# A planner's table of durations in a two-layer trunk (windowed attention, gated DeltaNet): measured times on all engines, a shared port, one load queue

## The chip, the core and the metric

The kernel runs on one core of one Trainium2 chip. A core has five engines that run their own instruction streams side by side: TensorE (PE in the profile; matmuls, with its weight loads shown as PEld), VectorE (DVE), ScalarE (ACT), GpSimd (POOL) and SyncE (SP), which issues the DMA transfers here. They meet only through semaphores. The metric is the device time of one execution in microseconds (us), given as the median of several runs; one further execution is recorded by the profiler.

## The reference

Two decoder layers over a prompt of 1024 tokens and a sample group of 8 sequences of 4 tokens, with 1024 features, all in float32. Each layer computes

```python
x = x + gate(c) * Branch(rms_norm(x) * (1 + scale(c)) + shift(c))
```

with shift, scale and gate from `silu(c) @ w_mod + b_mod`. Every branch has one input projection, which also yields a gate path z, and one output projection of `branch_output * silu(z)`.

Layer 0's branch is attention with 16 query and 4 key heads of 64: each query sees itself and the 128 positions before it (a learned sink per head joins the softmax); the sample group's queries see a cache of 128 positions. Layer 1's branch is gated DeltaNet: q, k and v pass a causal convolution over 4 tokens and SiLU, q and k are normalised, and each of 16 value heads (two to a q/k head) carries a 128 x 128 state S:

```python
S_t = exp(g_t) * S_{t-1} + k_t u_t^T
u_t = beta_t * (v_t - (exp(g_t) * S_{t-1})^T k_t)
o_t = S_t^T q_t / sqrt(128)
```

It is done by chunks: inside a chunk a unit lower triangular system is solved, and a scan over the chunks carries S. After the layers a last norm follows. Outputs are the tokens of both groups, the new key and value caches, the new convolution tails and the new states.

## The kernel before, in words

**Tiling.** Tokens lie on the free axis during projections: 1056 tokens (1024 + 32) in groups of 384, 384 and 288. A float32 product of full precision is made of three matmuls on operands split in a high and a low part: `wh x hhi`, `wh x hlo`, `wl x hhi` (rows `ps_pj<-h2hi,wh` and so on in the profile). Weights come in by DMA (`wr`), ScalarE rounds them to `wh` and GpSimd subtracts to get `wl`.

**Layer 1.** The 16 value heads are 8 pairs, `hq` 0 to 7. For each pair there are: `solve` (L1834), which builds the triangular blocks of eight chunks of 128 tokens in tiles UZ; `invert` (L1884), which inverts all 32 x 32 diagonal blocks of a pair at once on VectorE, in a tile X, in 31 steps of two instructions (`tmp<-X`, a product, and `X<-X,tmp`, a subtraction; the 31 pairs are the 62 instructions of which the prediction speaks); `diagonal` and `blocks` (L1938), which put these inverses back (`Xd`, VectorE's STREAM_TRANSPOSE into UZ) and build the off-diagonal blocks by small matmuls (`ps_lg<-UZ,M`) that VectorE copies into UZ; `decayed`, `chain` (L1986), the scan over the eight chunks, in each of which a matmul with UZ gives u, VectorE scales it to `us`, TensorE multiplies it with k (`ps_mi<-us,ktok`), and VectorE updates S; `output` and `gating` (`vo`, `mo`, `zl`). Before the last stage (the output projection, `out_y_p<-xt`) come the sample group's states, `S<-in_state_gdn_s`, which are loaded once for products with q and k (KQT, cK, cQ) and once more for their update.

**What sets the order of the work.** The program is written by Python generators, here called jobs. `weave(gen, name, hq)` (L487) puts a job in a list sorted by a rank out of the tables `K` and `KR` (L241). After each projection matmul `stages()` (L498) resumes every job whose condition is true; `until(cond)` (L509) stops the projections until a condition holds, and resumes only jobs. Conditions are of two kinds: counts (`finished[0] >= r - 1`, L2173: the chain of pair r - 1 is done before the k projection of pair r + 1 goes on), and times of a planner. The planner is the class `Core`: each instruction issued through it passes a helper (L89, the line that nearly all rows of the profile bear), and `Core.issued` (L111) adds its estimated duration to a clock `free[engine]` and notes when each tile was `written` and last `used`. `ready(tile)` holds when the tile's planned time is not after TensorE's clock, `soon(tile)` allows 0.4 us and `idle(engine, tile)` 0.8 us beyond. In the order in which they are issued the instructions are then bound, engine by engine, by dependencies with the reason "program order". So the planner's durations don't alter any instruction; they decide where each one stands in its engine's stream. The inversion's steps, for example, each wait on `yield idle("vector")`.

The durations before, in short: a fixed part and a rate for each engine (VectorE 0.08 us and 960 elements per us and partition, GpSimd 0.02 or 0.14 us and 420, a DMA 2.4 us whatever its size), with 0.1 us from an instruction to the next that needs it on the same engine and 0.2 us to another engine.

`cached` (L1036) is the job that opens the sample group's attention against the cache (loads `kc`, `vc`) once the prompt's attention is done.

## Time and profile before

| | |
|---|---|
| runs: median (lowest to highest) | 1736.98 us (1735.34 to 1741.25), 3 runs |
| the profiled execution | 1732.34 us |
| its span on the core | 1730.6 us |
| TensorE busy | 1621.2 us (94%), 10666 instructions |
| VectorE, ScalarE, GpSimd busy | 1174.6, 862.6 and 675.5 us |
| mean granted TensorE clock | 0.982 |
| moved by DMA | 191.82 MB |

Rows of the profile read: start, duration, engine, line, operation, `out<-in`, partitions x elements, count; a bracket at the end gives the time that the engine had stood idle before, and what released it. In rows of a wait the three numbers are total time, times and longest. Rows by stretch of time give, for each engine, the busy time and the count of instructions in it. TensorE's matmuls are pipelined, so that a duration can be longer than the distance to the next start.

### The profile page before, as it was taken

What the parts mean: (1) busy time and instruction counts of PE and PEld (TensorE: products, weight loads), DVE (VectorE), ACT (ScalarE), POOL (GpSimd) and SP (SyncE); (2) the same over time, 40 slices, a digit from 0 to 9 for tenths busy, and PEclk for the clock granted to TensorE, in tenths of its full rate; (3) what the DMA queues carried; (4) which work ended last, traced back from release to release, by engine and by line L of the source; (5) the groups of instructions that cost most, each with busy time, mean ns of one, the idle gap of its engine ahead of it and who ended that gap; (6) DMA issues with size and microseconds to landing.
All of it is one profiled execution on the core that took longest, in us unless ns stands there. A gap on an engine that the chain in (4) does not pass through costs nothing. (4 is left out here: it accounts for less than half of the span.)

```text
span 1730.6 us, 32224 instructions
## 1 busy us (share of the span) xinstructions
PE 1621.2 (94%) x10666; PEld 1429.5 (83%) x10666; DVE 1174.6 (68%) x3538; ACT 862.6 (50%) x2514; POOL 675.5 (39%) x1576
## 2 busy tenths in 40 slices
PE   6999999999999999589999999999999998989897
PEld 5987888977788889469989999899999996657675
DVE  4426675555565787757878778778697776357676
ACT  5625555453335664166554655554655655332332
POOL 2601121122213356235544654546356565323332
PEclk9999999999999999799999999999999999999998
DMA  9542122234233323122412324224132237764885
GB/s 330 153 133 73 51 58 55 51 103 114 92 122 97 105 55 85 29 68 69 127 42 73 102 58 114 65 69 117 46 104 70 56 93 227 218 190 138 244 268 171
DMA packets 281577, 191.82 MB, mean 111 GB/s; under 512 B 98361, under 2 KB 253881, under 8 KB 281378
## 3 DMA queue, kind: packets, MB, share of 16 engines
q1 hardware_dynamic: 281410, 189.75, 38.2%
q8 instruction: 85, 1.39, 0.3%
q14 instruction: 82, 0.67, 0.1%
HBM read 144.68 MB, written 47.04 MB: 111 GB/s over the span
## 5 line engine op out<-in xcount | busy, mean ns | idle before, releaser
L89 POOL TENSOR_TENSOR wl<-wr,wh 128x128 fp32r<-128x128 f32 x488 | 236.7, 515 | 485.5 <-ACT wh L89 449.4
L89 PE MATMUL ps_pj<-h2hi,wh 128*128 128x384 f32 (+1 forms) x1128 | 379.9, 337 | 0.0
L89 PE MATMUL ps_pj<-h2lo,wh 128*128 128x384 f32 (+1 forms) x1128 | 378.1, 335 | 0.0
L89 PE MATMUL ps_pj<-h2hi,wl 128*128 128x384 f32 (+1 forms) x1128 | 376.8, 334 | 0.0
L89 PEld LDWEIGHTS ps_pj<-h2hi,wh 128*128 128x128 f32 x1128 | 213.2, 189 | 3.1 <-ACT wh L89 0.2
L89 PEld LDWEIGHTS ps_pj<-h2hi,wl 128*128 128x128 f32 x1128 | 213.2, 189 | 2.7 <-POOL wl L89 0.2
L89 PEld LDWEIGHTS ps_pj<-h2lo,wh 128*128 128x128 f32 x1128 | 213.0, 189 | 2.2
L89 POOL TENSOR_TENSOR xt<-xt,y 128x512 f32<-128x512 f32 (+1 forms) x48 | 63.6, 1328 | 194.3 <-DVE y L89 170.4
L89 PE MATMUL ps_pj<-hlo,wh 128*128 128x384 f32 (+1 forms) x360 | 119.1, 331 | 0.0
L89 PE MATMUL ps_pj<-hhi,wh 128*128 128x384 f32 (+1 forms) x360 | 118.4, 329 | 0.0
L89 PE MATMUL ps_pj<-hhi,wl 128*128 128x384 f32 (+1 forms) x360 | 118.1, 328 | 0.0
L89 DVE SCALAR_TENSOR_TENSOR vT<-XR,cT,vT 128x384 f32<-128x384 f32 (+1 forms) x144 | 83.9, 591 | 47.4 <-ACT vT L89 45.3
L89 DVE TENSOR_TENSOR tmp<-X 64x31 f32<-64x31 f32 (+15 forms) x248 | 89.0, 359 | 16.9 <-POOL X L89 13.4
L89 DVE TENSOR_TENSOR X<-X,tmp 64x31 f32<-64x31 f32 (+15 forms) x248 | 90.7, 366 | 8.5
L89 ACT CAST wh<-wr 128x512 fp32r<-128x512 f32 x122 | 75.1, 617 | 16.4 <-PE ps_pj L89 11.3
L89 POOL TENSOR_TENSOR Xd<-Xc,cst 32x128 f32<-32x128 f32 x128 | 62.7, 490 | 40.5 <-DVE UZ L89 24.4
L89 PEld LDWEIGHTS ps_pj<-hlo,wh 128*128 128x128 f32 x360 | 67.7, 188 | 10.5 <-issue 10.5
L89 ACT COPY XR<-ps_pj 128x384 f32<-128x384 f32 (+1 forms) x96 | 43.0, 448 | 59.5 <-PE ps_pj L89 59.4
L89 PEld LDWEIGHTS ps_pj<-hhi,wh 128*128 128x128 f32 x360 | 67.7, 188 | 4.0 <-issue 3.1
L89 ACT ACTIVATE prob<-prob,nm 128x256 f32<-128x256 f32 (+1 forms) x128 | 62.2, 489 | 15.5 <-DVE nm L89 15.3
L89 PEld LDWEIGHTS ps_pj<-hhi,wl 128*128 128x128 f32 x360 | 67.7, 188 | 2.2 <-issue 2.1
L89 ACT ACTIVATE qe<-ps_mi,Eg 128x128 f32<-128x128 f32 x112 | 34.9, 363 | 60.4 <-PE ps_mi L89 60.3
(574 smaller groups left out, 4203.9 us busy)
## 6 DMA issues: line engine op xcount, KB each, us to landing
wr<-in_gdn_w_in SPq DMA_DIRECT2D x96, 256.0 KB
S<-in_state_gdn_s SPq DMA_DIRECT2D x40, 256.0 KB
xt<-in_x_prompt SPq DMA_DIRECT2D x16, 512.0 KB
wm<-in_w_mod SPq DMA_DIRECT2D x16, 512.0 KB
wr<-in_swa_w_in SPq DMA_DIRECT2D x64, 128.0 KB
wmod<-in_w_mod SPq DMA_DIRECT2D x32, 256.0 KB
wm<-in_w_mod SPq DMA_DIRECT2D x32, 256.0 KB
DP<-gcr SPq DMA_DIRECT2D x64, 128.0 KB
```

Of the source, the lines that this page charges most:

```text
L89: inst = fn(*args, **kwargs)
```

## The change

`Core` prices instructions in a new way; nothing else but one condition is touched.

- `issued` calls a function for each engine. `on_tensor`: 0.174 us for 384 columns in the fast format (0.164 before), 0.14 us more where tiled and untiled matmuls change over, double durations for the first 4 us after TensorE has been idle for over 2.2 us, and 0.165 us until the result is there. `on_scalar`: smaller fixed parts, 0.09 us for a scale or bias per partition, 0.093 for an accumulated sum, 1.29 us to change the function table, 0.1 us until the result. `on_vector`: other fixed parts, the double rate for all `tensor_scalar` forms from SBUF, 0.08 us until the result, and an instruction with two operands from SBUF (or at the double rate) starts only after a GpSimd instruction that is planned to run at that time. `on_gpsimd`: memsets have a price, and an instruction starts only after such a VectorE instruction.
- Loads and stores share one queue in the planner: each takes a time by its size and its longest run of adjacent bytes, and lands no sooner than 2.0 us after it starts.
- The step from one instruction to the next that needs it is `GO`, 0.035 us (0.05 from a DMA, none from TensorE to TensorE), in place of 0.1 and 0.2.
- `cached` also waits until the job `modulate` is over.

```diff
--- before.py
+++ after.py
@@ -76,6 +76,9 @@
 CONST, COFF = constants()
 
 
+GO = 0.035
+
+
 class Engine:
 
 
@@ -100,7 +103,8 @@
         self.tc, self.nc = tc, tc.nc
         self.free, self.last = {}, {}
         self.written, self.used, self.slots, self.parts, self.wide = {}, {}, {}, set(), {}
-        self.group = 0
+        self.group, self.full, self.slow, self.table, self.queue = 0, True, 0.0, 0, 0.0
+        self.pool, self.port = [], []
         for e in ("tensor", "scalar", "vector", "gpsimd", "sync"):
             self.free[e] = 0.0
             setattr(self, e, Engine(self, e))
@@ -115,42 +119,106 @@
         n = 1
         for d in outs[0].shape[1:]:
             n *= d
-        start = self.free[eng]
+        start = base = self.free[eng]
         for a in srcs:
             start = max(start, self.after(self.written, a, eng))
             if a.space == PSUM:
                 start = max(start, self.after(self.used, a, eng))
         for a in outs:
-            if self.used.get(self.key(a), (0.0, ""))[1] != "sync" or eng != "sync":
-                start = max(start, self.after(self.used, a, eng))
+            t, e = self.used.get(self.key(a), (0.0, eng))
+            if e != eng or eng not in ("tensor", "sync"):
+                start = max(start, t + GO)
         if "dma" in op:
+
             self.free[eng] = start + 0.45
-            end = start + 2.4
+            size = outs[0].shape[0] * n if outs[0].space != DRAM else int(np.prod(outs[0].shape))
+            part = min(4 * self.run(outs[0]), 4 * self.run(srcs[0]), 4096)
+            self.queue = max(self.queue, start + 0.9) + size * 4 / part * (8.5 + part * 0.0375) * 7e-5
+            end = done = max(start + 2.0, self.queue + 1.0)
         else:
-            rate, fixed = {"tensor": (2400 if op == "matmul" and srcs[0].dtype == F32R
-                                      else 1200 if op == "transpose" else 600, 0.004),
-                           "scalar": (1200, 0.06 if op == "copy" and srcs[0].space == PSUM else 0.14
-                                      if srcs and srcs[0].space == PSUM else 0.18),
-                           "vector": (960, 0.13 if op == "scalar_tensor_tensor" else 0.08),
-                           "gpsimd": (420, 0.02 if n >= 256 else 0.14)}[eng]
-            if op == "matmul" and outs[0].shape[0] <= 64 and srcs[0].dtype == F32:
-                rate = 2400 if n <= 64 and outs[0].shape[0] <= 32 else 600 * P / outs[0].shape[0] if self.group != outs[0].offset // outs[0].ap[0][0] else rate
-            if eng == "tensor":
-                self.group = outs[0].offset // outs[0].ap[0][0]
-            if op == "tensor_scalar_mul" and srcs and srcs[0].space != PSUM and eng == "vector":
-                rate = 1920
-            if op == "memset":
-                rate = 1e9
-            end = self.free[eng] = start + fixed + n / rate
+            start, dur, late = getattr(self, "on_" + eng)(op, start, base, n, outs, srcs, args, kwargs)
+            self.free[eng], end, done = start + dur, start + dur + late, start + dur + 0.02
             if eng in self.last:
                 self.tc.add_manual_dep(ins, self.last[eng],
                                        mybir.DependencyInfo(mybir.DependencyClass.NoSync, mybir.DependencyReason.DATA),
                                        reason="program order")
             self.last[eng] = ins.name
         for a in srcs:
-            self.used[self.key(a)] = max(self.used.get(self.key(a), (0.0, "")), (end, eng))
+            self.used[self.key(a)] = max(self.used.get(self.key(a), (0.0, "")), (done, eng))
         for a in outs:
             self.written[self.key(a)] = self.used[self.key(a)] = (end, eng)
+
+    @staticmethod
+    def run(a):
+
+        r = 1
+        for step, count in reversed(list(a.ap) if a.space == DRAM else list(a.ap)[1:]):
+            if count == 1:
+                continue
+            if step != r:
+                break
+            r *= count
+        return r
+
+    def on_tensor(self, op, start, base, n, outs, srcs, args, kwargs):
+        if start - base > 2.2:
+            self.slow = 4.0
+        rows = outs[0].shape[0]
+        tiled = rows <= 64 and srcs[0].dtype == F32 and op == "matmul"
+        group = outs[0].offset // outs[0].ap[0][0]
+        if tiled:
+            dur = 2 * (n / 1200 + 0.004)
+            if group != self.group:
+                dur = max(0.014, dur * rows / P)
+        elif srcs[0].dtype == F32R:
+            dur = max(0.108, n / 2400 + 0.014)
+        else:
+            dur = (1 if op == "transpose" else 2) * max(0.108, n / 1200 + 0.003)
+        if tiled == self.full:
+            dur += 0.14
+        self.group, self.full = group, not tiled
+        half = min(dur, self.slow)
+        self.slow -= half
+        return start, dur + half, 0.165
+
+    def on_scalar(self, op, start, base, n, outs, srcs, args, kwargs):
+        fixed = 0.05 if srcs and srcs[0].space == PSUM else 0.095
+        if op == "activation":
+            func = args[2] if len(args) > 2 else kwargs.get("func")
+            table = 1 if func in (AF.Exp, AF.Tanh) else 2 if func == AF.Silu else 0
+            if table and table != self.table:
+                start += 1.29 if self.table else 0.0
+                self.table = table
+        if hasattr(kwargs.get("scale"), "tensor") or hasattr(kwargs.get("bias"), "tensor"):
+            fixed += 0.09
+        if kwargs.get("accum_out") is not None:
+            fixed += 0.093
+        return start, fixed + n / 1200, 0.1
+
+    def on_vector(self, op, start, base, n, outs, srcs, args, kwargs):
+        scaled = op.startswith("tensor_scalar")
+        rate = 1920 if scaled and (not srcs or srcs[0].space != PSUM) else 960
+        fixed = 0.13 if op == "scalar_tensor_tensor" or scaled and len(srcs) > 1 else 0.1 if op == "transpose" else 0.075
+        dur = 0.0 if op == "memset" else fixed + n / rate
+
+        ins = [a for a in args[1:] if hasattr(a, "tensor")] + [a for k, a in kwargs.items() if hasattr(a, "tensor") and k not in ("out", "accum_out")]
+        big = sum(a.space != PSUM and np.prod(a.shape[1:]) >= max(2, n // 2) for a in ins)
+        if big > 1 or big and rate == 1920:
+            for x, y in reversed(self.pool[-12:]):
+                if x <= start < y:
+                    start = y
+            self.port.append((start, start + dur))
+        return start, dur, 0.08
+
+    def on_gpsimd(self, op, start, base, n, outs, srcs, args, kwargs):
+        dur = 0.03 + n / 1150 if op == "memset" else 0.14 + n / 470 if n < 256 else 0.03 + n / 420
+        if op != "memset" and n < 256 and outs[0].shape[-1] == P and outs[0].dtype == F32R:
+            dur = 0.41
+        for x, y in self.port[-12:]:
+            if x <= start < y:
+                start = y
+        self.pool.append((start, start + dur))
+        return start, dur, 0.045
 
     def key(self, a):
 
@@ -160,7 +228,7 @@
 
     def after(self, table, a, eng):
         t, e = table.get(self.key(a), (0.0, eng))
-        return t + (0.0 if e == eng == "tensor" else 0.1 if e == eng else 0.2)
+        return 0.0 if e == eng == "tensor" else t + (0.05 if e == "sync" else GO)
 
     def slot(self, key, bufs, t):
 
@@ -1036,7 +1104,7 @@
         def cached():
 
             nonlocal sa_guard, sa
-            yield lambda: attended[0] == 4 * NB
+            yield lambda: attended[0] == 4 * NB and over("modulate")()
             at_guard.__exit__(None, None, None)
             open_wo(4)
             sa_guard = tc.tile_pool(name="sa", bufs=1, side="left")
```

## The prediction

> **What bounds the kernel now.** I read the page first, then the busy time of each engine stage by stage, then what TensorE waited for.
>
> ```profile
> span 1730.6 us, 32224 instructions
> PE 1621.2 (94%) x10666; PEld 1429.5 (83%) x10666; DVE 1174.6 (68%) x3538; ACT 862.6 (50%) x2514; POOL 675.5 (39%) x1576
> ...
> PE   6999999999999999589999999999999998989897
> ```
>
> TensorE (PE) is busy for 94% of the span, so the program is TensorE work plus the holes in it. Time that a new order can win lies in the holes; each digit of the second row is 43 us, and only slice 17 (692 to 735 us) is clearly low.
>
> ```profile
> core 0: us, PE busy (x) PEld busy (x) DVE busy (x) ACT busy (x) POOL busy (x), PEclk, DMA share, GB/s
> 628.00:633.00 5.00, 4.44 (x23) 4.44 (x24) 4.64 (x12) 4.48 (x16) 0.00 (x0) 0.67 0.04 7
> ...
> 691.00:708.30 17.30, 0.38 (x11) 0.29 (x10) 15.62 (x43) 0.00 (x0) 2.75 (x7) 0.55 0.13 33
> 708.30:762.00 53.70, 46.04 (x373) 35.72 (x368) 34.46 (x98) 19.94 (x73) 15.99 (x57) 0.92 0.21 53
> 762.00:1100.00 338.00, 328.25 (x2286) 311.96 (x2284) 263.28 (x756) 193.87 (x608) 178.95 (x503) 0.99 0.31 83
> 1100.00:1540.00 440.00, 422.54 (x2875) 377.18 (x2876) 311.46 (x872) 241.03 (x742) 217.27 (x575) 0.99 0.41 114
> ...
> 1600.00:1731.00 131.00, 111.16 (x497) 87.09 (x494) 91.09 (x293) 40.44 (x93) 37.70 (x29) 0.95 0.75 228
> ```
>
> From 762 to 1540 us TensorE is 96 to 97% busy: no order of the same matmuls can win much there (778 - 751 = 27 us of holes in all). From 691 to 708.3 it does nothing while VectorE (DVE) is busy for 15.6 of 17.3 us; and the last 131 us have 20 us of holes with the DMA engines 75% busy. What TensorE waited for in these places:
>
> ```profile
> PE ps_lg L89 <- DVE UZ L89: 19.0, 6, 16.9
> ...
> PE ps_mi L89 <- ACT kb L89: 6.8, 4, 3.3
> ...
> PE ps_lg L89 <- DMA S<-in_state_gdn_s: 5.3, 3, 2.3
> PE ps_lg L89 <- DVE KQT L89: 4.4, 1, 4.4
> ...
> PE ps_lg L89 <- ACT kT L89: 3.6, 2, 3.3
> PE ps_mi L89 <- DMA kc<-in_cache_swa_k: 3.2, 2, 2.7
> ```
>
> (The columns are total, times, longest.) One wait, 16.9 us on UZ, is by far the largest that the planned part has. All other rows are under 7 us.
>
> **The change: what it moves.** Only the planner's durations and one condition change, so the instructions stay the same: TensorE 9031, VectorE 3540, ScalarE 2083, GpSimd 1581 in the planned program before and after, in the same counts by kind. The DMAs go from 1121 to 1119 (two 256 KB state loads become one of 512 KB, and so do two stores). TensorE's switches between projection matmuls and other work fall from 1103 to 1093, those into or out of tiled matmuls from 313 to 309: nothing to price. What is left is who stands ahead of whom, and I compared both orders engine by engine.
>
> **The stage at 681 to 758 us.** Here the loop over head pairs has no projections left to issue: `until(finished[0] >= r - 1)` (L2173) holds the next pair's k projection until the chain of pair 0 is done. VectorE is the engine that everyone waits for:
>
> ```profile
> 680.86 0.18 DVE L89 TENSOR_TENSOR tmp<-X 64x31 f32<-64x31 f32 x1 [2.00 <-POOL X L89]
> ...
> 690.83 0.55 DVE L89 TENSOR_TENSOR X<-X,tmp 64x240 f32<-64x240 f32 x1
> ...
> 693.16 0.56 DVE L89 TENSOR_TENSOR X<-X,tmp 64x252 f32<-64x252 f32 x1
> ...
> 696.91 0.41 DVE L89 TENSOR_TENSOR X<-X,tmp 64x252 f32<-64x252 f32 x1
> ...
> 706.31 0.18 DVE L89 TENSOR_TENSOR X<-X,tmp 64x31 f32<-64x31 f32 x1
> 706.42 0.60 DVE L89 SCALAR_TENSOR_TENSOR DP<-ps_lg,sj,DP 128x128 f32<-128x128 f32 x2
> 706.94 0.69 DVE L89 STREAM_TRANSPOSE UZ<-Xd 128x512 f32<-128x512 f32 x1
> ...
> 716.06 0.61 DVE L89 TENSOR_SCALAR us<-ps_ob,sd 128x128 f32<-128x128 f32 x2
> ...
> 737.26 0.61 DVE L89 TENSOR_SCALAR us<-ps_ob,sd 128x128 f32<-128x128 f32 x2
> ...
> 740.13 0.61 DVE L89 SCALAR_TENSOR_TENSOR vo<-ps_mi,nEg,vo 128x128 f32<-128x128 f32 x2 [0.86 <-PE ps_mi L89]
> ...
> 741.32 0.61 DVE L89 TENSOR_SCALAR us<-ps_ob,sd 128x128 f32<-128x128 f32 x2 [0.25 <-PE ps_ob L89]
> ...
> 755.04 0.61 DVE L89 TENSOR_SCALAR us<-ps_ob,sd 128x128 f32<-128x128 f32 x2 [0.25 <-PE ps_ob L89]
> ```
>
> From 680.86 to 706.5 VectorE runs the 62 inversion steps (tmp/X) of pair 1, with only one transposition of pair 0 among them; pair 0's other three transpositions, its UZ copies and its chain (first `us` at 716.06) stand behind them, though pair 0 is the one that TensorE needs:
>
> ```profile
> 708.01 1.06 PE L89 MATMUL ps_lg<-UZ,M 128*32 128x64 f32 x16 [16.92 <-DVE UZ L89]
> ...
> 758.16 0.42 PE L89 MATMUL ps_pj<-h2hi,wh 128*128 128x384 f32 x1
> 758.43 0.33 PE L89 MATMUL ps_pj<-h2lo,wh 128*128 128x384 f32 x1
> 758.60 0.34 PE L89 MATMUL ps_pj<-h2hi,wl 128*128 128x384 f32 x1
> ```
>
> In the changed order the inversion starts at the same place of VectorE's program (instruction 1326 against 1324), but pair 0's transpositions come at 1332, 1344, 1353 and 1359 (before: 1326, 1389, 1393, 1397) and its first `us` at 1360 (before: 1398). So 24 inversion steps stand ahead of the chain, the other 38 go between its eight steps in twos and fours, and pair 1's own blocks (64 small matmuls) come at the end of the chain, partly beside projections. New time of the first `us`: the 24 steps take 680.86 to 691.38, three transpositions more 3 x 0.69 = 2.1, the copies and DP some 3 us: 696.5, if they fill each other's waits for TensorE; with some of those left (716.06 - 706.94 = 9.1 us now holds about 4.5 of waiting), 699. Then the chain: undisturbed it takes 741.32 - 737.26 = 4.1 to 4.4 us a step ((755.04 - 741.32)/3 = 4.6 with a little other work). The 38 steps left take 706.5 - 691.4 = 15.1 us, 2.2 for each of seven intervals; VectorE is idle there for about 0.86 + 0.25 and, ahead of S, another 0.8 = 1.9 us. The holes aren't where the steps fall, so I add 1 us to each interval: 7 x 5.4 + 3.1 (755.04 to 758.16) = 41, and the projections resume at 740 instead of 758: a gain of 18 us.
>
> Of it I take off the work that only moves: 64 matmuls of the kind of the row at 708.01 (1.06/16 = 0.066 us) are at most 4.2 us, at least 2.8; 3.5. And the inversion now stands 8 VectorE instructions later and pair 0's block matmuls 27 projection matmuls later on TensorE (4.6 us at the 0.17 us from 758.43 to 758.60, all of it useful work and so no loss by itself, but the chain begins that much later): 2 us. Net -12.5; between -17 and -4 (each interval stretched by the whole 2.2 us, chain starting at 702).
>
> **TensorE's clock.**
>
> ```profile
> 628.56 0.47 PE L89 MATMUL ps_lg<-cst,kT 128*128 128x128 f32 x1 [3.27 <-ACT kT L89]
> ...
> 629.48 0.52 PE L89 MATMUL ps_pj<-h2lo,wh 128*128 128x384 f32 x1
> 629.80 0.52 PE L89 MATMUL ps_pj<-h2hi,wl 128*128 128x384 f32 x1
> ```
>
> After the 3.27 us wait projections follow each other at 0.32 us (629.48 to 629.80), and the granted clock of 628 to 633 is 0.67; after the 16.9 us it is 0.92 over 708 to 762. So a long wait costs its length and 1 to 2 us after it. In the changed order 64 projection matmuls stand between the turning of the rows and this kT transposition, against 39: 25 x 0.17 = 4.3 us more cover for a wait of 3.27. I take -4 (the wait, and about 0.7 for the slow matmuls after it), between -5 and 0.
> The Trainium skill, "TensorE: Matmul & The Clock Gate", section "What's actually happening", has the array fall to half clock only after an idle window of about 3.4 us. By that rule a wait of 3.27 us need not cost the clock, and the sum would be 1723; the two rows at 629 show half speed, so the trace decides.
>
> **The rest.** The new condition `over("modulate")` on `cached` (L1039) lets the sample caches' loads wait for the last modulation. That now lies 24 TensorE instructions later (2123 against 2099), but the prompt's attention ends 47 earlier (2107 against 2154), and the loads of kc start 20 earlier: the 2.7 us wait on kc may shrink, at worst it stays; behind `cached` there are 61 projection matmuls as cover against 34. -1, between -3 and +3.
> The KQT wait (4.4 us, at 1558) stays: 8 matmuls of cover against 10, behind the same VectorE work. 0, to +1.
> Through 762 to 1540 us producers and consumers are packed a little closer: the TensorE work between `us` and the uo/DP matmul has, at the durations of such rows, a median of 0.82 us against 0.98, between prob and its transposition 1.13 against 1.26. The rows at 740.13 and 741.32 show such a hop at 0.25 to 0.86 us where nothing covers it; ten more of them would cost 6. +2, between -5 and +6.
> The tail: the sample states' updates start 52 TensorE instructions later (8514 against 8462) and end 47 earlier (8961 against 9008), with 68 plain output matmuls left at the end. Their 17 MB of loads and stores go through a window a fifth shorter, in a stretch that runs at 228 GB/s and a DMA share of 0.75:
>
> ```profile
> 1610.19 6.67 DMA of<-gTd
> ...
> 1701.75 6.13 DMA out_y_p<-xt
> ```
>
> Against it, the last chain may lose a wait on kb (3.3 us) or on S. 0, between -6 and +9.
>
> **Sum.** -12.5 - 4 - 1 + 0 + 2 + 0 = -15.5 on a profiled execution of 1732.3 us (span 1730.6 and 1.7 around it): 1717. The median of the runs, 1736.98, stands 4.6 above the profiled one; I carry that over: **1722 us**.
>
> **The rivals.**
> *VectorE is the bound of that stage anyway, so nothing is won.* Its work from 681 to 755 doesn't shrink, and GpSimd gets in its way: the same X step takes 0.56 us while GpSimd works (693.16) and 0.41 without it (696.91).
>
> ```profile
> L89 POOL TENSOR_TENSOR wl<-wr,wh 128x128 fp32r<-128x128 f32 x488 | 236.7, 515 | 485.5 <-ACT wh L89 449.4
> ```
>
> In the new order the last 38 steps run beside the chain's GpSimd work: 38 x 0.15 = 5.7 us, 0.8 an interval; and if every step also delays a link of the chain by its whole length (2.2 an interval), the projections resume at 699 + 7 x (4.4 + 2.2 + 0.8) + 3.1 = 754. That is a gain of 4, less the 5.5 taken off above: +1.5; with the other terms 1735, no change. For it speaks that VectorE is 90% busy in 691 to 708; against it that it is 64% busy in 708 to 762 and the steps can wait for holes.
> *The two engines lock each other out.* If a step that meets a GpSimd instruction waited for the whole of it (0.515 us in the mean by the row above), 38 steps would lose 20 us instead of 5.7: 1749. The 0.15 us above speak against it. The Trainium skill, "SBUF — State Buffer", section "SBUF: two separate sides", states this rule, for VectorE operations with two SBUF inputs against GpSimd ones that read SBUF.
> *Slower: the tail waits for its loads.*
>
> ```profile
> 1667.90 5.63 DMA xt<-x2d
> ...
> 1707.89 2.40 DMA xt<-x2d
> ```
>
> Loads of the same 512 KB take 5.63 us to land among the state transfers and 2.40 at the end. If the state transfers of the sample, a fifth closer together, put 3.2 us ahead of the loads of each of the eight output blocks, and nothing covers it, the tail grows by 26 us: 1748. Five blocks (16 us) undo the forecast, seven make it slower. For it speaks the DMA share of 0.75; against it that some blocks wait that long already, and that the updates end sooner.
> *Larger gain.* If the new order also takes the waits on kb, S and KQT (6.8 + 5.3 + 4.4 = 16.5 us) down by two thirds, another 11 us go: 1711. The order around KQT speaks against it.
>
> **How the numbers follow.** Forecast (1712 to 1730) 0.53, larger gain 0.11, no change (1732 to 1742) 0.14, lock 0.05, slower by the tail 0.17. Two runs of this kernel can differ by 0.3%, 5 us, which I take as the bound of "same". Faster: forecast, larger gain and the fringe of no change, 0.67; same 0.11; slower 0.22. The range of 8 in 10 cuts a tenth at each end: 1706 (the larger gain with the stage near its bound of -17) to 1744.
>
> **What would show it.** In the profile after: the wait of TensorE on UZ at about 690 falls from 16.9 to under 5 us; X steps stand between `us` rows; projections resume 56 to 64 us after the inversion's first step, not 77; the kT wait of 3.3 us is gone; slices 18 to 36 stay at 9. I am wrong if the `us` rows stand 6.5 us apart or more, if new waits of 3 us and more appear between 760 and 1540 us, or if the last 131 us have grown, with DMA rows in their chain.

## The result, and the profile after

The changed kernel takes 1748.15 us (median of 10 runs, 1741.53 to 1754.11); the kernel before takes 1737.96 us beside it (10 runs, 1735.34 to 1743.45). The ratio is 1.0052, interval [1.0034, 1.0069]: half a per cent slower. The forecast was 1722 us, faster, and its range (1706 to 1744) doesn't hold the median.

The profiled execution of the changed kernel took 1741.53 us, the shortest of its ten, 6.6 us under their median; that of before took 1732.34, 5.6 under its median. The traces can be compared with each other, but neither stands for a median.

From the page of the changed kernel, the span, the busy time and TensorE's 40 slices:

```profile
span 1739.7 us, 32252 instructions
PE 1633.6 (94%) x10666; PEld 1428.4 (82%) x10666; DVE 1181.3 (68%) x3538; ACT 861.5 (50%) x2514; POOL 679.8 (39%) x1576
...
PE   6999999999999999799999999999999998996997
```

Slice 17 has risen from 5 to 7, as forecast. But TensorE's busy time has grown by 12.4 us for the same 10666 matmuls, and slice 37 has fallen from 9 to 6. What TensorE waits for now (total, times, longest):

```profile
PE ps_pj L720 <- DMA xt<-in_x_prompt: 9.6, 1, 9.6
PE ps_lg L92 <- DVE oH L92: 9.2, 1, 9.2
PE ps_mi L92 <- DVE us L92: 7.4, 8, 1.7
PE ps_tr L92 <- ACT vT L92: 7.0, 8, 2.2
PE ps_mi L92 <- ACT uo L92: 6.8, 8, 3.0
PE ps_tr L92 <- ACT vo L92: 6.5, 7, 3.8
PE ps_mi L92 <- ACT kb L92: 5.3, 3, 3.6
...
PE ps_lg L92 <- DVE UZ L92: 2.3, 7, 0.6
```

(L92 is the helper that was L89. The first row is the start, before any planned work.) The UZ wait of 16.9 us is gone, and so are those on KQT (4.4) and kT (3.3). New are one of 9.2 us on oH, in the sample group's part of layer 1, and many short ones.

**Stage by stage.** A wait's place says little when all the work has moved. So I cut both traces at the same projection matmuls: the k-th `ps_pj` matmul is the same one in every order. The stretches of before, and behind them those of after with the same projections in them:

```profile
core 0: us, PE busy (x), PEclk, DMA share, GB/s
681.63:773.00 91.37, 63.40 (x491) 0.87 0.21 53
773.00:1347.47 574.47, 560.58 (x3959) 1.00 0.30 80
1347.47:1439.24 91.77, 90.97 (x642) 1.00 0.32 89
1439.24:1582.64 143.40, 129.23 (x686) 0.95 0.70 207
1582.64:1625.26 42.62, 36.32 (x158) 0.96 0.63 193
1625.26:1717.84 92.58, 90.60 (x413) 1.00 0.77 232
```

```profile
core 0: us, PE busy (x), PEclk, DMA share, GB/s
675.66:756.99 81.33, 68.16 (x502) 0.90 0.26 69
756.99:1341.96 584.97, 565.94 (x3958) 1.00 0.30 78
1341.96:1446.29 104.33, 97.74 (x676) 0.98 0.27 79
1446.29:1575.61 129.32, 120.43 (x629) 0.99 0.73 218
1575.61:1631.16 55.55, 40.28 (x178) 0.85 0.53 158
1631.16:1728.53 97.37, 92.08 (x414) 1.00 0.76 235
```

Up to the first cut the new order is 6.0 us ahead, and in the stage of the forecast another 10.0. Then it loses 10.5 us over 585 with the same matmuls, although the clock is 1.00 in both. Of these, 5.1 are holes that the profile shows (19.0 against 13.9); the other 5.4 are counted as busy. A projection matmul's bar is 0.34 us and the next one starts 0.17 later, so a hole of up to 0.17 us isn't seen as idle, and waits too short for the table above can hide in them. How much of the 5.4 they are can be estimated from the distances from start to start, each against the median of the same pair of matmuls in all kept traces: delays of over 0.34 us have grown by 4.7 us (19 of them in place of 14), shorter ones by 3.5 (336 in place of 302), and 1.9 come of other neighbours. The next two stretches have to be read together, since 34 matmuls more stand in the first and 57 fewer in the second: +12.6 and -14.1. The fifth has 15.3 us of holes against 6.3, the wait on oH; the last is 4.8 us longer. From 773 on the sum is +26.7 us, and the whole +10.7 at the last matmul.

How far one execution can be trusted shows a later run: experiment 3's first kernel has the same order as the changed one up to about 1535 us. Its differences to before, in the first four stretches from the start, are -0.2, -12.8, +15.2 and +12.5 us, where the changed kernel has -6.0, -10.0, +10.5 and +12.6. So a stretch is known to some 5 us, no better.

### The profile page after: what moved, and what is told of

Its sections match the earlier page's. It is cut to its first block, busy times and chain, and to the rows that moved or that the text cites. A ratio compares the mean times of both kernels' runs of the same rounds, so it can differ in the third digit from the quotient of the medians.

```text
span 1739.7 us, 32252 instructions
## 1 busy us (share of the span) xinstructions
PE 1633.6 (94%) x10666; PEld 1428.4 (82%) x10666; DVE 1181.3 (68%) x3538; ACT 861.5 (50%) x2514; POOL 679.8 (39%) x1576
## 5 line engine op out<-in xcount | busy, mean ns | idle before, releaser
L92 POOL TENSOR_TENSOR wl<-wr,wh 128x128 fp32r<-128x128 f32 x488 | 241.2, 524 | 509.2 <-ACT wh L92 441.0
L92 PE MATMUL ps_pj<-h2hi,wh 128*128 128x384 f32 (+1 forms) x1128 | 379.5, 336 | 0.0
L92 PE MATMUL ps_pj<-h2lo,wh 128*128 128x384 f32 (+1 forms) x1128 | 379.3, 336 | 0.0
L92 PE MATMUL ps_pj<-h2hi,wl 128*128 128x384 f32 (+1 forms) x1128 | 377.8, 335 | 1.6 <-POOL wl L92 1.6
L92 PEld LDWEIGHTS ps_pj<-h2hi,wl 128*128 128x128 f32 x1128 | 213.2, 189 | 4.4 <-POOL wl L92 2.0
L92 PEld LDWEIGHTS ps_pj<-h2hi,wh 128*128 128x128 f32 x1128 | 213.6, 189 | 3.3 <-ACT XR L92 0.4
L92 PEld LDWEIGHTS ps_pj<-h2lo,wh 128*128 128x128 f32 x1128 | 213.2, 189 | 2.7
L92 POOL TENSOR_TENSOR xt<-xt,y 128x512 f32<-128x512 f32 (+1 forms) x48 | 63.3, 1321 | 214.4 <-DVE y L92 184.5
L92 PE MATMUL ps_pj<-hlo,wh 128*128 128x384 f32 (+1 forms) x360 | 119.8, 333 | 0.0
L92 PE MATMUL ps_pj<-hhi,wh 128*128 128x384 f32 (+1 forms) x360 | 118.5, 329 | 0.2 <-DVE kll L92 0.2
L92 PE MATMUL ps_pj<-hhi,wl 128*128 128x384 f32 (+1 forms) x360 | 118.1, 328 | 0.0
L92 DVE SCALAR_TENSOR_TENSOR vT<-XR,cT,vT 128x384 f32<-128x384 f32 (+1 forms) x144 | 84.1, 595 | 46.6 <-ACT vT L92 44.5
L92 DVE TENSOR_TENSOR X<-X,tmp 64x31 f32<-64x31 f32 (+15 forms) x248 | 89.3, 360 | 8.5
L92 DVE TENSOR_TENSOR tmp<-X 64x31 f32<-64x31 f32 (+15 forms) x248 | 87.5, 353 | 10.1 <-POOL X L92 6.5
L92 ACT CAST wh<-wr 128x512 fp32r<-128x512 f32 x122 | 75.1, 617 | 9.8 <-PE ps_pj L92 8.4
L92 PEld LDWEIGHTS ps_pj<-hlo,wh 128*128 128x128 f32 x360 | 67.9, 189 | 10.6 <-issue 10.6
L92 ACT ACTIVATE prob<-prob,nm 128x256 f32<-128x256 f32 (+1 forms) x128 | 62.3, 490 | 19.5 <-DVE nm L92 19.3
L92 ACT ACTIVATE vo<-vo,fo 128x128 f32<-128x128 f32 x128 | 41.9, 392 | 60.4 <-POOL fo L92 60.4
L92 PEld LDWEIGHTS ps_pj<-hhi,wh 128*128 128x128 f32 x360 | 67.8, 188 | 4.0 <-issue 3.5
L92 PEld LDWEIGHTS ps_pj<-hhi,wl 128*128 128x128 f32 x360 | 68.0, 189 | 2.7 <-issue 2.3
L92 POOL TENSOR_TENSOR rst<-rsw 128x4 f32<-128x4 f32 x96 | 25.3, 263 | 113.8 <-DVE rsw L92 100.6
L92 ACT COPY XR<-ps_pj 128x384 f32<-128x384 f32 (+1 forms) x96 | 43.0, 448 | 50.6 <-PE ps_pj L92 50.1
```

What stands on the lines that cost most here:

```text
L92: inst = fn(*args, **kwargs)
```

## Experiments

Each kernel was timed beside the kernel before, whose medians in these calls were 1734.75 to 1736.12 us. None leaves work out. Where I give a "row of stretches", it holds the seven differences from the profile of before, cut as above (start to 681.63, then the six stretches). They are of one execution each, with the uncertainty just shown.

**1. The stage by itself.** Before, with only the inversion of pair 1 held back after 12 of its 31 steps until pair 0's blocks are done (`solved` counts those pairs):

```diff
             for k in range(31):
+                if hq == 1 and k == 12:
+                    yield lambda: solved[0] >= 1
```

> The kernel before, with one wait for the order alone: the inversion of pair 1 stops after 12 of its 31 steps until pair 0's blocks are solved (as many steps ahead of the chain as in the changed kernel). Nothing else is edited. If the block of inversion steps ahead of pair 0's copies is what the 16.9 us were, the wait on UZ falls under 3 us, the projections resume 12 to 18 us earlier and the kernel takes 1724 to 1730 us, 8 to 14 below the kernel before; the loss of the change then lies wholly in other places, some 20 us of it. If VectorE bounds that stage whatever the order (the rival of the prediction), it takes 1735 to 1740.

1726.41 us, ratio 0.9956 [0.993, 0.9981]. Row of stretches: +3.8, -11.6, +3.4, +1.4, -3.1, +0.1, -1.9. Its profile:

```profile
PE ps_lg L89 <- DVE UZ L89: 4.8, 7, 1.7
...
747.47 0.42 PE L89 MATMUL ps_pj<-h2hi,wh 128*128 128x384 f32 x1
```

The long UZ wait is gone, the projections resume at 747.47 (before 758.16), and the gain reaches the end: 8.8 us between the medians. So the gain of this stage is real, and the stretch itself is 11.6 us shorter where 12.5 was forecast. That the changed kernel doesn't show it is due to what comes later.

Held after 10 steps instead of 12:

```diff
+                if hq == 1 and k == 10:
+                    yield lambda: solved[0] >= 1
```

> The kernel before with the inversion of pair 1 stopped after 10 steps in place of 12: two steps (four instructions of about 0.42 us) less ahead of the chain of pair 0, so its start comes 1 to 2 us earlier, and as much more between the chain's steps. The wait on UZ stays under 3 us. By the stage alone 1724 to 1728 us, like the first experiment (1726); it tells whether that gain holds for a neighbouring order, and is a candidate for the fastest version.

**1723.42 us**, ratio 0.9936 [0.9917, 0.9954], the fastest kernel of this study, ahead of both. Row: +2.5, -13.0, -4.0, +2.7, -0.8, +1.5, -1.8.

**2. Is it scatter?** If small moves in the order cost as much as this result, no cause is to be found in it. So I moved the orders by prices that mean nothing: before with VectorE's fixed part 0.085 instead of 0.08, before with GpSimd's rate 415 instead of 420.

```diff
-                           "vector": (960, 0.13 if op == "scalar_tensor_tensor" else 0.08),
+                           "vector": (960, 0.13 if op == "scalar_tensor_tensor" else 0.085),
```

```diff
-                           "gpsimd": (420, 0.02 if n >= 256 else 0.14)}[eng]
+                           "gpsimd": (415, 0.02 if n >= 256 else 0.14)}[eng]
```

> A control: the kernel before, with one of the planner's fixed VectorE prices at 0.085 us in place of 0.08, a change that says nothing true or false of the chip. If the tables of ranks and positions fit the old prices so closely that any other order loses, it is slower by 4 us or more (1742 to 1755). If an order is as good as another, it stays within 3 us of 1738, and the loss of the change has causes of its own.

> A second control on the kernel before: GpSimd's rate in the planner at 415 in place of 420 elements per us, which again says nothing of the chip. If the first control was no accident and the old order is one picked out among many, this is slower than the kernel before too, by 5 to 20 us (1741 to 1756). If the first was an accident, 1732 to 1740.

1747.69 us (1.0072 [1.0057, 1.0087]) and 1746.95 us (1.0066 [1.004, 1.0091]): either one costs about as much as the whole change. The same on the changed kernel, VectorE's fixed part 0.08 instead of 0.075, ScalarE's 0.1 instead of 0.095:

```diff
-        fixed = 0.13 if op == "scalar_tensor_tensor" or scaled and len(srcs) > 1 else 0.1 if op == "transpose" else 0.075
+        fixed = 0.13 if op == "scalar_tensor_tensor" or scaled and len(srcs) > 1 else 0.1 if op == "transpose" else 0.08
```

```diff
-        fixed = 0.05 if srcs and srcs[0].space == PSUM else 0.095
+        fixed = 0.05 if srcs and srcs[0].space == PSUM else 0.1
```

> A control on the changed kernel: one fixed VectorE price at 0.08 us in place of 0.075. If orders made with the new durations scatter as the old ones do, and the changed kernel is one of them, this lands anywhere in 1740 to 1765 us. If the new durations are worse for a reason of their own, it stays close to the changed kernel, 1745 to 1752.

> A second control on the changed kernel: one fixed ScalarE price at 0.1 us in place of 0.095. As with the one before: by scatter anywhere in 1740 to 1765 us, and in the mean of these two, the changed kernel and the two edits tried before (1757, 1765) above the controls on the kernel before only if the new durations themselves are worse; by a cause of the new durations' own 1745 to 1752.

1742.15 us (1.0049 [1.0032, 1.0067]) and 1743.73 us (1.0055 [1.0035, 1.0074]): by the ratios, where the changed kernel was. But the stretch of the forecast gains only 3.5 and 4.1 us in them, though no wait on UZ is over 0.9 us. And the two moved orders of before with the hold of experiment 1:

> The second control (old prices, GpSimd's rate at 415; 1747 us) with the first experiment's edit: the inversion of pair 1 stops after 12 steps until pair 0's blocks are solved. If the two effects stand side by side, it gains what the kernel before gained by that edit, 9 to 12 us: 1735 to 1739. That is below the changed kernel (1748) and its two controls (1742, 1744), which have the interleaved inversion too: by 3 to 13 us the new durations then order the rest worse than the old ones. If it stays above 1742, the gain of the stage is itself used up by whatever order follows it, and the rest is no worse with the new durations.

> The same edit on the first control (old prices, a fixed VectorE price at 0.085; 1748 us). By two effects side by side 1736 to 1740; if an order's scatter is as large as the gain, anywhere in 1735 to 1755.

1729.09 us (0.9967 [0.995, 0.9985]) and 1748.93 us (1.0091 [1.0071, 1.011]). In the second the stage takes 5.4 us less than before (3.8 more without the hold), and the next stretch gives it back (+9.0, where it is -1.9 without the hold).

Last, the hand-made ranks of the jobs, which might fit the old prices alone, turned round for pairs 2 to 7 in both planners (with the hold in the old one):

```diff
+    KR = KR[:2] + KR[3:] + KR[2:3]
```

> The first experiment (old prices, inversion of pair 1 stopped after 12 steps; 1726 us) with the ranks of pairs 2 to 7 passed on by one. If the tables' fit to the old prices is what the old orders have ahead of the new ones, it goes lost here: 1740 to 1755 us. If the old prices give better orders by themselves, it stays at 1722 to 1735.

> The changed kernel (1748 us) with the same ranks passed on by one. By the tables' fit it stays where it was, 1740 to 1756, and beside the run before it; if the new prices are worse by themselves it is 12 us or more above that run.

1734.61 us (1.0005 [0.9992, 1.0017]), 8 us over experiment 1, and 1753.43 us (1.0097 [1.0072, 1.0123]), 5 us over the changed kernel. If the ranks' fit to the old prices made the difference, the gap should have closed; it was 22 us and is 19. That is one pair of orders, and such pairs scatter.

So five orders by the old prices, all with the stage mended, give 1723, 1726, 1729, 1735 and 1749 us, and four by the new ones 1742, 1744, 1748 and 1753. The means are 1732 and 1747, and the groups overlap by one (1749). Where the two groups part, in the mean of four rows each (experiments 1 and 11 with the hold, the moved one at 1729, the other ranks; and the four new ones): +4.2, -12.5, +0.5, +2.7, -0.1, +0.6, -1.7 against -3.5, -7.1, +9.8, +11.3, -12.2, +12.4, +4.1. The order at 1749 is left out of the first mean; with it that mean is +5.6, -11.1, +2.2, +2.1, +0.2, +0.4, -1.6.

The loss between 773 and 1347 us and that behind 1582 are in all four new orders, but the first is also in the order at 1749 (+9.0) and in part in the other ranks (+4.9). What parts the groups without overlap is the sum from 1347 us to the end: 12.2 to 20.9 us in the four new orders, -3.6 to 4.5 in all five old ones. Even that isn't proof of a cause: the moved order with GpSimd's 415, without the hold, has 17.7 there, most of it at another place (+13.6 before 1439).

**3. Which wait?** The 9.2 us on oH: the sample group's core starts later on VectorE in the new order, and TensorE arrives at its result early. I let the job `core` go first (`core=4` to `core=0` in the table K):

```diff
-... states=21, core=4, new=9)
+... states=21, core=0, new=9)
```

> The changed kernel with the rank of the sample group's core at 0 in place of 4, so that its VectorE instructions (copies of qd, cQ, cK) stand ahead of the output projection's splits and gathers; the order up to about 1440 us stays the same. If the wait on oH (9.2 us, with 3.6 us on kb behind it) is lost time, it falls to about 3 us and the kernel takes 1739 to 1743 us, 5 to 9 below the changed one. If the end is bound by something else (the sample states' transfers and updates), the waits only move to kb and S and the time stays within 3 us of 1748.

1749.25 us (1.0081 [1.006, 1.0102]). The wait does shrink, and others grow:

```profile
PE ps_lg L92 <- DVE oH L92: 3.4, 1, 3.4
```

The row ends on -9.4, +4.3, +10.8 where the changed kernel has -14.1, +12.9, +4.8: 8.6 us are won at oH, and 4.7 and 6.0 lost before and behind it. So taking the wait on oH down doesn't give its time back.

If the loss is in short waits, TensorE comes to results that the planner thinks are there. Four tries on the changed kernel. First, a longer step behind small GpSimd operations:

```diff
-        return start, dur, 0.045
+        return start, dur, 0.13 if n < 64 else 0.045
```

> The changed kernel, in whose planner a result of a small GpSimd instruction (under 64 elements) is there 0.13 us after its end in place of 0.045. In the profile after, the steps of the reciprocal root on GpSimd that makes fo follow each other at 0.32 us in the mean, where the new planner counts 0.23 and the old one counted 0.25; the transposition of vo waits for fo. If that price is what costs the time, the waits of ps_tr on vo (16 us over the usual distances between matmuls, 5.5 in the kernel before) fall to 8 or less and the kernel takes 1738 to 1742 us, 6 to 10 below the changed one. If the time lies elsewhere, or if a new price only shuffles the order anew, it stays at 1745 to 1755.

1757.15 us (1.0126 [1.0105, 1.0148]); it has more waits on us, 16.1 us instead of 7.4.

Second, no waits at the shared port:

```diff
             for x, y in reversed(self.pool[-12:]):
-                if x <= start < y:
+                if False:
                     start = y
...
         for x, y in self.port[-12:]:
-            if x <= start < y:
+            if False:
                 start = y
```

> The changed kernel, in whose planner VectorE and GpSimd don't wait for each other's ports any more; all else as changed. If the waits that the planner puts between the two engines are what delays the sample group's core and leaves TensorE the 9.2 us on oH and 3.6 us on kb at 1592 us, both are gone and the kernel takes 1733 to 1740 us. If the waits are real ones of the chip (copies of qd take 1.3 us instead of 0.27 beside GpSimd), the stall comes back at this or another place near 1590 and the time stays at 1744 to 1752.

1764.6 us (1.0177 [1.0152, 1.0203]): without the port waits the planner gives a worse order, with 10.6 us of waits on vT and 9.9 on us. So this part of the change isn't by itself the cause of the loss.

Third, 0.15 us more in `ready` for every result that no DMA wrote:

```diff
-        return max((self.after(self.written, t, "tensor") for t in ts), default=0.0)
+        return max((self.after(self.written, t, "tensor") + (0.15 if self.written.get(self.key(t), (0.0, "sync"))[1] != "sync" else 0.0) for t in ts), default=0.0)
```

> The changed kernel, in whose planner a result counts as ready for TensorE 0.15 us later than it would (loads excepted). If the new durations lose because TensorE's matmuls are put so close behind their producers that each small lateness is waited for, the waits on vo, uo and Xd (36 us over the usual distances between matmuls, 11 in the kernel before) fall by half or more and the kernel takes 1732 to 1742 us. If lateness isn't the cause, the margin costs what it adds, and it takes 1748 to 1760.

1751.4 us (1.0098 [1.0081, 1.0114]).

Fourth, TensorE's durations times 0.93:

```diff
-        return start, dur + half, 0.165
+        return start, 0.93 * (dur + half), 0.165
```

> The changed kernel with all of TensorE's new durations scaled by 0.93 in the planner: the margin of the old prices without their errors from one kind of matmul to another. By the hidden margin 1730 to 1740 us, like the run before it; if the margin does nothing, 1745 to 1760; if the two part by over 10 us, the scatter of orders is larger than what either tells.

1748.69 us (1.0061 [1.0039, 1.0082]); row -5.7, +1.1, +1.9, -5.8, +2.7, +9.2, +5.3. The middle loses only 1.9 us in this order, but the gain of the first stage is gone.

**4. Which part of the new prices?** The changed kernel with the old TensorE prices (`on_tensor`'s body replaced):

```diff
+        rate = 2400 if op == "matmul" and srcs[0].dtype == F32R else 1200 if op == "transpose" else 600
+        if op == "matmul" and outs[0].shape[0] <= 64 and srcs[0].dtype == F32:
+            rate = 2400 if n <= 64 and outs[0].shape[0] <= 32 else 600 * P / outs[0].shape[0] if self.group != outs[0].offset // outs[0].ap[0][0] else rate
+        self.group = outs[0].offset // outs[0].ap[0][0]
+        return start, 0.004 + n / rate, 0.165
```

> The changed kernel with the old prices of TensorE's instructions (all else new). The planned program's TensorE work is then reckoned some 8% too short, so that what runs beside it is placed earlier in TensorE's terms, and each producer gets more cover than the planner thinks. If the old order owed its rest to that hidden margin, 1730 to 1740 us. If not, 1745 to 1760, with the first chain's stage still mended.

1765.76 us (1.0181 [1.0156, 1.0207]).

And with the old DMA price:

```diff
-            size = outs[0].shape[0] * n if outs[0].space != DRAM else int(np.prod(outs[0].shape))
-            part = min(4 * self.run(outs[0]), 4 * self.run(srcs[0]), 4096)
-            self.queue = max(self.queue, start + 0.9) + size * 4 / part * (8.5 + part * 0.0375) * 7e-5
-            end = done = max(start + 2.0, self.queue + 1.0)
+            end = done = start + 2.4
```

> The changed kernel with the old price of a transfer, 2.4 us whatever its size and its neighbours. If the queue of loads in the planner is what holds work back (states of the sample group, which wait for loads that it reckons late, and with them the core and oH), the wait on oH is gone and the kernel takes 1728 to 1740 us. If the queue tells the truth, the planner is blind without it where loads take 5 to 7 us to land (the last 130 us), and new waits on S, of and xt bring the time to 1746 to 1760.

1738.24 us (1.0011 [0.9996, 1.0026]), 10 us better than the changed kernel: the tail is as before (-0.6, -1.6, -0.6 at the end of its row; oH waits 0.5 us), the middle is not (+13.9, +4.8). That would make the load queue the cause of the loss in the tail. With VectorE's fixed part 0.08 on top (the edit of group 2):

> The same, with a fixed VectorE price at 0.08 us in place of 0.075 (as in the first control on the changed kernel): a second order with the old price of transfers. It should stand within 5 us of the run before it if that price is the cause of what it shows; if only scatter was seen, the two lie 10 us or more apart, or on both sides of 1745.

1760.07 us (1.0136 [1.0119, 1.0153]), 22 us more, by one price changed by 0.005 us. Its row ends on -0.3, +8.7, -0.4, +2.1, so here too the stretch at oH is as before; but the stretch up to 1347 takes 20.4 us more. A single order can't tell that a price is right or wrong.

One thing holds in every order that was profiled. The wait on oH is 0.5 us in both orders with the old DMA price and 0.3 to 0.5 in all eight by the old prices; it is 9.2 in the changed kernel, its three neighbours (moved twice, and the other ranks) and the kernel with the longer GpSimd step, and 1.8 to 7.9 in the other five with the new DMA price. So the price of the load queue brings that wait into the order. It doesn't follow that it costs as much: from 1347 us to the end the two orders with the old DMA price lose 2.0 and 10.1 us, the four new ones 12.2 to 20.9.

## Why the prediction was wrong

**The stage at 681 to 758 us: right in mechanism, and in size partly by luck.** Forecast was a first `us` at 699, steps of 5.4 us, projections again at 740, net -12.5 us. VectorE and TensorE of the changed kernel:

```profile
679.50 0.18 DVE L92 TENSOR_TENSOR tmp<-X 64x31 f32<-64x31 f32 x1 [4.85 <-POOL X L92]
...
695.59 0.61 DVE L92 TENSOR_SCALAR us<-ps_ob,sd 128x128 f32<-128x128 f32 x2
696.55 0.41 DVE L92 TENSOR_TENSOR X<-X,tmp 64x247 f32<-64x247 f32 x1
...
702.55 0.59 DVE L92 TENSOR_SCALAR us<-ps_ob,sd 128x128 f32<-128x128 f32 x2
...
736.78 0.61 DVE L92 TENSOR_SCALAR us<-ps_ob,sd 128x128 f32<-128x128 f32 x2
...
740.11 0.42 PE L92 MATMUL ps_pj<-h2hi,wh 128*128 128x384 f32 x1
```

The X steps stand between the `us`, which are (736.78 - 695.59)/7 = 5.9 us apart, and the projections resume at 740.11, 60.6 us after the inversion's first step. The stretch gained 10.0 us in this profile and 11.6 in the experiment that does it alone. The rival "VectorE is the bound of that stage" falls. Two misses nearly cancel: the first `us` came 16.1 us after the inversion's first step where 18.1 was forecast, and the seven intervals were 3.4 us longer in all. Also, the bound of -4 doesn't follow from its own terms: 702 + 7 x (4.4 + 2.2) + 3.1 = 751, a gain of 7, less the 5.5 taken off is 1.5. The two moved new orders gained 3.5 and 4.1.

**The clock and the caches: right in direction, the size not shown.** The kT wait is gone, and the time up to 681.63 is 6.0 us shorter where -4 and -1 stood; but in the three neighbours of the changed kernel it is 4.6, 2.1 and 1.1 shorter, in the run with the same order 0.2, and a start that waits for its first load is in it.

**"Through 762 to 1540 us producers and consumers are packed a little closer ... +2, between -5 and +6": wrong, this step failed first.** Between 773 and 1347 the same matmuls took 10.5 us more. I had looked for waits by the largest ("no order of the same matmuls can win much there"), and an order can't win much there, but it can lose. TensorE's matmul on uo, in that stretch, before and after (duration, then idle time before it and how often):

```profile
L89 PE MATMUL ps_mi<-uo,DP x160: 270/275/377, 809.7 to 1293.8; 128*128 128x128 f32 x160
its engine sat idle before it (us, times) until:
  ACT uo L89: 1.1, 1
```

```profile
L92 PE MATMUL ps_mi<-uo,DP x160: 270/275/377, 796.4 to 1284.5; 128*128 128x128 f32 x160
its engine sat idle before it (us, times) until:
  ACT uo L92: 5.2, 5
```

The same 160 matmuls wait five times instead of once, 4.1 us more. The distances that I took from the two orders (0.82 against 0.98 us ahead of uo) pointed there; the size, +2 where 10.5 came, was wrong. I had priced ten more hops of up to 0.86 us. What came was in good part a few longer waits: the longest on uo is 3.0 us, and a new one of 2.1 us on Xd stands in the same stretch. The prediction's own sign of being wrong, new waits of 3 us and more between 760 and 1540 us, came with this one at 1028 us and one of 3.8 us on vo at 1412.

**The tail, "0, between -6 and +9": wrong.** From 1347 to the end the new order lost 16.2 us. "The KQT wait (4.4 us, at 1558) stays" was wrong: it went. In its place came oH, which I did not have:

```profile
1601.09 1.09 PE L92 MATMUL ps_lg<-cst,oH 128*128 128x128 f32 x4 [9.21 <-DVE oH L92]
```

I priced the tail by DMA volume and looked at the queue; the sample group's core on VectorE, whose copies `qd` start 7.6 us later (1538.23 against 1530.59, rows below) while TensorE is 7.0 us ahead by the cut at 1582.64, stood in the changed order: by the planner's own times TensorE waits 9.1 us there, so this could have been read before the run. The rival "slower: the tail waits for its loads" gave 1748, the time that came, but not by its mechanism: in the last stretch TensorE waits for no load.

**The sum.** By the profiles the forecast was -15.5 and the result +9.2: 24.7 us off. The first stages (-16.0 where -17.5 stood) give 1.5 of it, the middle 8.5 (+10.5 for +2), the tail 16.2 (for 0); behind the last matmul the new order wins 1.5 back.

**What stays open.** Why the better clock gives worse orders isn't settled. It is better: the planner's first to last matmul is 1561 us for 1620 on the chip, 1447 for 1608 by the old prices. Each group of prices undone by itself gave another order and another time, from 1738 to 1766, and neighbours scatter by up to 22 us. What is shown is this: the located gain is 10 to 14 us in six of these nine orders and 3.5 to 5.4 in three; the rest of the order is drawn anew, at a scatter about as large; and the order of before stands 12 us better than its two moved neighbours. A change of the planner may give these 12 us up, but need not, as the moved order at 1729 shows. That four new-price orders lie on average 15 us above five mended old-price ones is a tendency, with one of the five among them. It is located in part, behind 1347 us, and the wait on oH in it goes back to the price of the load queue; the rest of the mechanism wasn't found.

## What to carry to other kernels

When a change redraws the order of a whole program, one located gain has to be weighed against the scatter of all the rest: measure that first, by moving a price that means nothing (here 0.005 us in one fixed part moved the time by 12 and 22 us). If one wait carries the gain, take it away by itself: two lines gained 0.6% where the better planner lost 0.5%. And where an engine is 97% busy, ask what an order can lose there, also in waits too short to be seen as idle. Last, a planner that writes down its own waits shows some of the losses before any run: 9.1 us here.

## What the runs showed of the hardware

**VectorE and GpSimd hold each other up, by microseconds in the operations on 128 partitions.** VectorE's four copies of 128x128 beside a GpSimd operation of 128x512, in the changed kernel, and then the same four copies in the kernel before, where GpSimd is idle:

```profile
1538.19 1.29 POOL L92 TENSOR_TENSOR wlB<-wr,whB 128x512 fp32r<-128x512 f32 x1 [5.22 <-ACT whB L92]
1538.23 3.02 DVE L92 COPY qd<-qk 128x128 f32<-128x128 f32 x4
```

```profile
1530.59 0.85 DVE L89 COPY qd<-qk 128x128 f32<-128x128 f32 x4
```

And the other way round, GpSimd behind VectorE, in a chain for whose end (vo) TensorE waits 3.76 us:

```profile
1406.68 0.21 POOL L92 TENSOR_TENSOR rsw<-rst,rsw 128x4 f32<-128x4 f32 x1
1406.96 2.24 POOL L92 TENSOR_TENSOR rst<-rsw 128x4 f32<-128x4 f32 x1
1407.01 1.92 DVE L92 SCALAR_TENSOR_TENSOR vT<-XR,cT,vT 128x384 f32<-128x384 f32 x4
...
1411.71 1.21 PE L92 MATMUL ps_tr<-cst,vo 128*128 128x128 f32 x4 [3.76 <-ACT vo L92]
```

A step of 0.2 us took 2.24, so about 2 of the 3.76 us are this delay. The Trainium skill, "SBUF — State Buffer", section "SBUF: two separate sides", says that the one that starts first holds the shared port for its whole instruction, and the other is blocked. These rows agree that one is blocked; they don't show who goes first, since the GpSimd bar begins 0.05 us ahead of the four VectorE instructions and ends only behind all four. My rival by this rule had the place wrong: the X steps of 64 partitions go on losing about 0.15 us (0.56 against 0.41 in the prediction's rows), and the big operations lose microseconds; why the short steps lose so little isn't shown. By the traces, VectorE instructions that take over 0.4 us longer than the median of their like number about 30 in the orders by the new prices and about 20 in before and its held neighbours (some 26 us against 16): the prices that reckon with the lock don't meet it less often.

**The clock can fall after a wait of 2.18 us and stay after one of 3.00.** The same instruction in the same order, once in the changed kernel and once in the kernel with the core first:

```profile
617.57 0.44 PE L92 MATMUL ps_pj<-h2hi,wl 128*128 128x384 f32 x1 [1.63 <-POOL wl L92]
...
618.03 0.34 PE L92 MATMUL ps_pj<-h2lo,wh 128*128 128x384 f32 x1
618.21 0.34 PE L92 MATMUL ps_pj<-h2hi,wl 128*128 128x384 f32 x1
```

```profile
621.86 0.55 PE L92 MATMUL ps_pj<-h2hi,wl 128*128 128x384 f32 x1 [2.18 <-POOL wl L92]
622.21 0.52 PE L92 MATMUL ps_pj<-h2hi,wh 128*128 128x384 f32 x1
622.53 0.52 PE L92 MATMUL ps_pj<-h2lo,wh 128*128 128x384 f32 x1
```

After 1.63 us the matmuls follow at 0.18 us, after 2.18 us at 0.32, for 3.4 us, which costs about (0.32 - 0.18)/0.32 x 3.4 = 1.5 us. But the length of the wait doesn't decide alone. In the changed kernel the clock stays at 1.00 behind this one:

```profile
1028.52 0.71 PE L92 MATMUL ps_mi<-uo,DP 128*128 128x128 f32 x4 [3.00 <-ACT uo L92]
```

In the kernel with the core first the same wait is 3.10 us, and the clock is 0.50 for 6.8 us. In all kept traces the granted clock is either full or half and changes in steps of 3.41 us, and what decides for the most part is how long TensorE was busy in the step before. Around the 2.18 us (stretch, PE busy, PEclk, DMA share, GB/s):

```profile
618.63:622.04 3.41, 1.23 (x7) 1.00 0.00 0
622.04:625.46 3.42, 3.42 (x12) 0.50 0.31 81
```

Cut into such steps, the 20 kept traces have 154 at full clock in which TensorE was busy for under 40%: the next step ran at half every time. From 40 to 60% that happened 91 times of 221, from 60% on 12 of 9327 times. So a wait of 2 to 3 us costs the clock or not by where it falls in the steps: 3.00 us lay across two (45% and 66% busy). The Trainium skill, "TensorE: Matmul & The Clock Gate", section "What's actually happening", has the clock halved after an idle window of about 3.4 us, in windows that run freely. The trace agrees with the window's length; the window needn't be idle throughout, 36% busy were too few here.
